# A hybrid diffusion layer: feature loads six tiles ahead, the left token block's down product in all eight banks, and weight sums formed one item early

## The chip, the cores and the metric

The kernel runs on one core of a Trainium2 chip. The metric is the device time of one execution in microseconds, the median of several runs. TensorE (PE) does the matrix products, with its weight loads shown as PEld; VectorE (DVE) and ScalarE (ACT) do the elementwise work; GpSimd (POOL) does one tiny power per row block; SyncE (SP) issues every DMA of the part spoken of here, in program order.

## The reference, cut to what matters

The layer is: a SwiGLU feed-forward block, a mixer of neighbourhood attention and a state-space scan with an output projection, and a second SwiGLU block, each followed by a residual and a layer norm. The change touches the end of the mixer (its last norm) and the whole second feed-forward block:

```python
def swiglu(h, w_up, w_down):
    a, g = jnp.split(h @ w_up, 2, axis=-1)
    return (jax.nn.silu(g) * a) @ w_down

x = post_norm(x, mod[5] * y, ln_g[layer, 1], ln_b[layer, 1])
x = post_norm(x, 0.5 * mod[8] * swiglu(modulate(x, mod[6], mod[7]), ffn2_w_up[layer], ffn2_w_down[layer]),
              ln_g[layer, 2], ln_b[layer, 2])
```

There are 1024 tokens and 1024 features in float32; the hidden width is 2816, that is 22 tiles of 128 features.

## The kernel before, in words

**Three matmuls for one.** Every float32 operand is split into a high part (ACT copies it into the matmul's format) and a low part (DVE subtracts that copy from the source; the helper `split`, L132 to L134). A product is high·high, high·low and low·high: L321 to L323 where weights are the stationary side (`mm3`), L381 to L383 where hidden features are (`token_major`).

**The weight stream.** `units` is the list of weight pieces of 128x1024 in the order of their use; `items` is the list of 128x512 operands made from them. `w_next` (L204) loads the next unit by an SP DMA into one of three `ws` buffers (some of the second block's up weights into two more, called `HX`). `w_split` (L229) makes the split of the next items, up to `ahead[0]` (usually 4) items beyond the one that PE takes now, into rings of four `wh` and four `wl` buffers; `apart` gives an item a place of its own outside the ring. `take` (L250) hands items to PE. All of this is written out in program order: an engine works through its own instructions in that order, so an instruction that waits holds up whatever stands behind it on the same engine.

**The up product of the second block.** It is computed with seven products in place of eight, over two halves of the input features, two column blocks (a and g of one hidden tile) and two token blocks of 512 (left and right). Four of a tile's seven items are plain halves of weights (1, 2, 4) or sums and differences of them: `s1` to `s4` in `seven` (L160), formed by DVE in a 128x1024 buffer `row` and then split as any other item. `ORDER` (L188) lists the (tile, item) pairs; for tiles 0 and 1 the seven are interleaved, because the right token block's sums (`RB`) are still being made then. That stretch is called the ramp here: `ramp(n)` after the n-th product runs `right1` (n = 2, 3), `right2` (n = 4, 5), `right3` (n = 6), `right4` and `right5` (n = 7). They transpose the normed right tokens on PE and form and split the block's sums on DVE and ACT. The left block's features that they need, spilled to DRAM as `xf` by `left_part`, come back by four DMAs (L1528, L1529) after the mixer's output projection. From tile 2 on, PE runs the products one after another; `gated` writes each finished hidden tile to DRAM (`hd`), high and low part, 1 MB a tile.

**The end of the mixer.** The output projection's right token block ends with `evac` (L1504): for each of four row tiles DVE multiplies by the gate (L1507), adds the residual (L1508), takes statistics (L401, L408, L410), waits for POOL's power (L411) and scales the tile (`normed`, L1494), which `turned_z` (L1544) transposes.

**The down product of the second block.** For each token block b (L1735), `token_major` runs over the two halves of the 1024 output columns, and in each over the 22 hidden tiles, with four banks (four row tiles) open at a time. All 22 hidden tiles of a block lie in SBUF (`hid_room`): `hid_load` (L1677) loads four of the left block's during the last products and the other 18 in one loop (L1700) before the first down product. After those stand the loads of the residual `z2` (L1708), two rows of norm parameters (L1711), two more (L1713). The work list `hi` has `resid2`, which DVE does in small steps when `pump` is called: z times a row (L1722), plus a row (L1724). The right block's hidden tiles replace the left's during the left block's second half (`follow`). At the end of each block every row tile's chain (L1751, L1752, statistics, POOL, L1739, L1740, store) is done at once as its banks finish (`out_now`). The weights of the down product are loaded twice, once for each token block.

```python
for j in range(4, NF):                     # L1700
    hid_load(0, j)
for t in range(4):                         # L1707
    dq.dma_start(z2[t], xh2[t])
for n, i in (("g1", 2), ("b1", 3)):
    rows[n] = rowt()
    row_load(rows[n], i)
hi += [resid2(z2[0:4]), more()]            # L1734
```

Of the kernel before, what the change touches and what calls it, by code (L numbers as in the profile page):

```python
# [48 lines left out]
def hybrid_layer(ctx: ExitStack, tc: tile.TileContext, I, out, dbg=None, stop=99):  # L49
# [110 lines left out]
    def seven(ua):  # L160
        ug = ua + 1
        h = lambda u, j: wst[u][:, j * 512:(j + 1) * 512]

        def s1():
            r = sums_of[ua] = rowt()
            V.tensor_tensor(r[:, 0:512], h(ug, 0), h(ug, 1), op=ALU.add)  # L166
            return r[:, 0:512]

        def s2():
            r = sums_of[ua][:, 0:512]  # L170
            V.tensor_tensor(r, r, h(ua, 0), op=ALU.subtract)
            return r

        def s3():
            r = sums_of[ua][:, 512:1024]
            V.tensor_tensor(r, h(ug, 0), h(ua, 0), op=ALU.subtract)
            return r

        def s4():
            r = sums_of.pop(ua)[:, 0:512]  # L180
# [14 lines left out]
    WO_END, U2 = len(items), len(units)  # L195
# [5 lines left out]
    plain(col("wd2", NF) * 2)  # L201


    def w_next(margin):  # L204
        u = pos[0]
        if u >= len(units) or (margin and u >= barred[0]):
            return False
        b = home[u][0] if u in home else turn_w[0] % NWS
        if b in owner and last_use[owner[b]] >= pos[1] - margin:
            assert margin, (u, b)  # L210
            return False
        if u in home:
# [5 lines left out]
        nc.sync.dma_start(w, units[u])  # L218
        wst[u] = w
        pos[0] += 1  # L220
        return True
# [6 lines left out]

    def w_split(n, must):  # L229
        while pos[1] < min(n, len(items)):  # L230
# [4 lines left out]
            u, f = items[i]  # L235
            if u >= barred[0] and i >= must:
                break
            w_dma(u + 1)
# [6 lines left out]
            split(wh, wl, f())  # L245
# [1237 lines left out]
    def more_units():  # L1483
# [6 lines left out]
        barred[0] = 10 ** 9  # L1490

    def normed(t, mv, rs):
        z = zz[4 + t]
        V.tensor_scalar(z, z, mv[:, 0:1], rs, op0=ALU.subtract, op1=ALU.mult)  # L1494
        dq.dma_start(xh2[4 + t], z)

    for b in range(2):
# [6 lines left out]
        def evac(hf_, t, p):  # L1504
# [3 lines left out]
            V.scalar_tensor_tensor(z, z, ALPHA, p, op0=ALU.mult, op1=ALU.add)  # L1508
            half_done(t, hf_, z)
# [16 lines left out]
    x11, x21 = pcs(ht, 0, 4), pcs(me, 0, 4)  # L1526
    for i in range(2):
        dq.dma_start(ht[:, i * 1024:(i + 1) * 1024], xf[i])  # L1528
        dq.dma_start(me[:, i * 1024:(i + 1) * 1024], xf[2 + i])  # L1529
# [8 lines left out]
          3: pair(hp[8:16]), 6: pair(hp[16:20] + ap_[0:4]), 7: pair(ap_[4:8] + spare)}  # L1538
# [28 lines left out]
    def right4(k):  # L1567
        V.tensor_tensor(x21[k], x21[k], t1f[k], op=ALU.subtract)

    def right5(k):  # L1570
        split(RB[4][0][k], RB[4][1][k], x21[k])
# [43 lines left out]
    def product(f, i):  # L1615
# [21 lines left out]
        if i == 4:  # L1637
# [9 lines left out]
    def ramp(n):  # L1647
# [6 lines left out]
        elif n == 6:  # L1654
            for k in range(4):
                right3(k)
        elif n == 7:
            for k in range(4):
                right4(k)
            hb4, a34 = slott("HB", [128, 6 * NB], F32R), slott("A3", [128, 1024], F32R)  # L1660
            RB[4] = pair(pcs(hb4, 0, 7) + pcs(a34, 0, 1))
            for k in range(4):
                right5(k)
            xe4 = slott("XE", [128, 4096])
            hring.extend([xe4[:, 0:2048], xe4[:, 2048:4096]])
# [34 lines left out]
    for j in range(4, NF):  # L1700
        hid_load(0, j)

# [3 lines left out]
    z2 = [ztile() for _ in range(4)]  # L1706
    for t in range(4):  # L1707
        dq.dma_start(z2[t], xh2[t])  # L1708
    for n, i in (("g1", 2), ("b1", 3)):
        rows[n] = rowt()  # L1710
        row_load(rows[n], i)  # L1711
    for i in range(2):
        row_load(fin[i], 4 + i)  # L1713
# [3 lines left out]
    for i in range(5):  # L1717
        apart[len(items) - 5 + i] = free[i][:, 0:512], free[i][:, 512:1024]

# [7 lines left out]
    def more():  # L1727
        for t in range(4):
            z2.append(slott(f"A{t}", [128, 1024]))
            dq.dma_start(z2[4 + t], xh2[4 + t])  # L1730
            yield None
        yield from resid2(z2[4:8])

    hi += [resid2(z2[0:4]), more()]  # L1734
    for b in range(2):  # L1735
        def out_now(t, mv, rs):
            z = z2[4 * b + t]
            for c in [slice(0, D)] if b == 0 or t < 3 else [slice(0, 512), slice(512, D)]:
                V.scalar_tensor_tensor(z[:, c], z[:, c], mv[:, 0:1], fin[0][:, c], op0=ALU.subtract, op1=ALU.mult)  # L1739
                V.scalar_tensor_tensor(z[:, c], z[:, c], rs, fin[1][:, c], op0=ALU.mult, op1=ALU.add)  # L1740
                dq.dma_start(out[4 * b + t][:, c], z[:, c])

        half_done, rest = norm(out_now)

        def src(f, t):
            return hid2[f][:, 0, t * 128:(t + 1) * 128], hid2[f][:, 1, t * 128:(t + 1) * 128]

        def evac(hf, t, p):
            c = slice(hf * 512, (hf + 1) * 512)
            z = z2[4 * b + t][:, c]  # L1750
            V.tensor_tensor(p, p, rows["g8"][:, c], op=ALU.mult)  # L1751
            V.scalar_tensor_tensor(z, z, ALPHA, p, op0=ALU.mult, op1=ALU.add)  # L1752
            half_done(t, hf, z)


        def follow():
            for _ in range(NF - 2):
                yield
            for f in range(NF):
                if f:  # L1760
                    hid_load(1, f - 1)
                yield

        fol = follow()
        token_major(NF, 4, src, evac, 2.0, (2, TAIL) if b else (2, 2), "dd", () if b else fol)
        if b == 0:
            for _ in fol:
                pass
            hid_load(1, NF - 1)
# [3 lines left out]
def layout(inp):  # L1773
# [15 lines left out]
    for i in (1, 2):  # L1789
        w = a[f"ffn{i}_w_up"][0].reshape(KD, 128, 2, NF, 128)  # L1790
        r[f"wu{i}"] = asc(w.transpose(3, 2, 1, 0, 4).reshape(2 * NF, 128, 1024))
        w = a[f"ffn{i}_w_down"][0].reshape(2, NF // 2, 128, 2, 512)
        w = w.transpose(0, 3, 1, 2, 4) if i == 1 else w.transpose(3, 0, 1, 2, 4)
        r[f"wd{i}"] = asc(w.reshape(NF, 2, 128, 512).transpose(0, 2, 1, 3).reshape(NF, 128, 1024))
    w = a["w_in"][0].reshape(KD, 128, 4, 4, 128).transpose(2, 3, 1, 0, 4).reshape(4, 4, 128, 1024)
# [48 lines left out]
```

## Time and the profile before

| | |
|---|---|
| median of 3 runs | 2274.38 us (2271.51 to 2275.09) |
| the profiled execution's own time | 2272.88 us |
| its span in the trace | 2271.0 us |
| PE busy | 2165.2 us, 95% of the span |
| DVE busy | 1595.5 us, 70% |
| ACT busy | 739.7 us, 33% |
| mean granted TensorE clock | 0.98 |

The span is the time from the first to the last instruction; the execution's own time is 1.9 us longer. PE's busy time is modelled and overlaps, so what counts below is where PE stands idle, and for what. All times of day are microseconds from the start of the span. The second feed-forward block's up product runs from about 1518 to 1970, its down product from 1970 to 2261.

### The profile page before, as it was taken

To read this page: it belongs to the slowest core of one execution; us is meant where nothing else is said; L and a number is where in the kernel's file an instruction comes from. 1 tells how busy PE (TensorE), PEld (TensorE's weight loads), DVE (VectorE), ACT (ScalarE), POOL (GpSimd) and SP (SyncE) were. 2 spreads that over 40 slices of the span, in tenths; PEclk is the share of its full clock that TensorE was granted. 3 is DMA by queue.
4 is the path that set the end of the run, shared out by engine and by line. 5 is a ranking of instruction groups with operands and counts; after the bars stand their busy time and mean duration, and the time that the engine had idled before them with its cause. 6 is when DMAs were issued, how large, how long until landed. Compare 5 with 4: busy or idle time off the path is not lost.

```text
span 2271.0 us, 32457 instructions
## 1 busy us (share of the span) xinstructions
PE 2165.2 (95%) x12272; PEld 1937.5 (85%) x12272; DVE 1595.5 (70%) x3421; ACT 739.7 (33%) x1547; POOL 24.6 (1%) x33
## 2 busy tenths in 40 slices
PE   7999999999999999999999899988999999959798
PEld 6998999889988999898999799865788888748686
DVE  7788788787888785554777467868777777543535
ACT  4322223423321333242223577234333333312121
POOL 0000000000000000000000000000000000000100
PEclk9999999999999999999999999998999999979899
DMA  9787623445444335227775871451333233485532
GB/s 344 254 295 247 253 75 117 140 168 167 124 139 131 113 125 171 93 103 240 253 250 187 202 169 37 170 208 48 130 112 112 111 112 112 160 302 190 209 102 83
DMA packets 166795, 372.30 MB, mean 164 GB/s; under 512 B 18152, under 2 KB 85736, under 8 KB 163824
## 3 DMA queue, kind: packets, MB, share of 16 engines
q1 hardware_dynamic: 166640, 370.25, 48.5%
q8 instruction: 96, 1.57, 0.3%
q14 instruction: 59, 0.48, 0.1%
HBM read 292.09 MB, written 84.06 MB: 166 GB/s over the span
## 4 chain that ended last, share of the span: by engine, by line
PE 81%; DVE 8%; DMA 5%; ACT 3%; issue 2%; SPq 1%; POOL 1%; POOLq 0%; ACTq 0%; DVEq 0%
PE pb L322 16%; PE pb L323 16%; PE pb L321 16%; PE pb L382 8%; PE pb L383 8%; PE pb L381 8%; PE pb L1337 2%; PE pb L1157 1%; DVE row L317 1%; PE pb L1312 1%; DVE wl L134 1%; ACT wh L133 1%; PE pb L1286 1%; PE pb L1287 1%; POOL rs L411 1%
## 5 line engine op out<-in xcount | busy, mean ns | idle before, releaser
L321 PE MATMUL pb<-X,wh 128*128 128x256 f32 (+2 forms) x1744 | 559.2, 321 | 1.1 <-ACT wh L133 1.1
L323 PE MATMUL pb<-X,wl 128*128 128x256 f32 (+2 forms) x1744 | 556.5, 319 | 0.0
L134 DVE TENSOR_TENSOR wl<-ws,wh 128x512 fp32r<-128x512 f32 x460 | 306.8, 688 | 267.2 <-ACT wh L133 264.8
L133 ACT ACTIVATE wh<-ws 128x512 fp32r<-128x512 f32 x460 | 281.1, 627 | 583.1 <-PE pb L383 362.0
L321 PEld LDWEIGHTS pb<-X,wh 128*128 128x128 f32 x1744 | 331.2, 190 | 10.3 <-ACT wh L133 2.0
L323 PEld LDWEIGHTS pb<-X,wl 128*128 128x128 f32 x1744 | 330.8, 190 | 9.3 <-DVE wl L134 0.9
L322 PE MATMUL pb<-X,wh 128*128 128x256 f32 (+2 forms) x946 | 307.5, 325 | 0.0
L322 PE MATMUL pb<-XT,wh 128*128 128x256 f32 (+2 forms) x886 | 284.6, 321 | 0.8 <-DVE XT L134 0.8
L381 PE MATMUL pb<-wh,HA 128*128 128x512 f32 x672 | 263.5, 392 | 2.6 <-DVE hid L350 2.1
L382 PE MATMUL pb<-wl,HA 128*128 128x512 f32 x672 | 261.5, 389 | 0.0
L322 PEld LDWEIGHTS pb<-X,wh 128*128 128x128 f32 x946 | 179.5, 190 | 7.1
L322 PEld LDWEIGHTS pb<-XT,wh 128*128 128x128 f32 x886 | 168.7, 190 | 7.4 <-DVE XT L134 2.8
L383 PE MATMUL pb<-wh,HA 128*128 128x512 f32 x416 | 162.0, 389 | 0.0
L321 PE MATMUL pb<-HA,wh 128*128 128x512 f32 (+2 forms) x424 | 154.4, 364 | 3.2 <-ACT wh L133 2.2
L323 PE MATMUL pb<-HA,wl 128*128 128x512 f32 (+2 forms) x424 | 153.3, 362 | 0.0
L381 PEld LDWEIGHTS pb<-wh,HA 128*128 128x128 f32 x672 | 126.2, 188 | 29.7 <-DVE hid L350 3.0
L382 PEld LDWEIGHTS pb<-wl,HA 128*128 128x128 f32 x672 | 126.2, 188 | 25.6
L322 PE MATMUL pb<-HA,wh 128*128 128x512 f32 (+2 forms) x336 | 118.7, 353 | 0.0
L134 DVE TENSOR_TENSOR wl<-row,wh 128x512 fp32r<-128x512 f32 x88 | 60.9, 693 | 73.3 <-ACT wh L133 73.3
L133 ACT ACTIVATE wh<-row 128x512 fp32r<-128x512 f32 x88 | 55.3, 628 | 172.1 <-DVE row L166 67.0
L383 PE MATMUL pb<-wh,HB 128*128 128x512 f32 x276 | 107.4, 389 | 0.0
L1611 DVE TENSOR_TENSOR z<-pb,z 128x512 f32<-128x512 f32 x154 | 105.7, 686 | 2.4 <-PE pb L323 0.7
(441 smaller groups left out, 3693.6 us busy)
## 6 DMA issues: line engine op xcount, KB each, us to landing
ws<-wu SPq DMA_DIRECT2D x122, 512.0 KB
ws<-wd SPq DMA_DIRECT2D x88, 512.0 KB
hd<-XE SPq DMA_DIRECT2D x22, 1024.0 KB
XE<-wada SPq DMA_DIRECT2D x36, 512.0 KB
HX<-wada SPq DMA_DIRECT2D x36, 512.0 KB
XE<-s5m SPq DMA_DIRECT2D x21, 768.0 KB
HA<-hd SPq DMA_DIRECT2D x20, 512.0 KB
HX<-wu SPq DMA_DIRECT2D x18, 512.0 KB
```

Source lines behind the costliest of these rows:

```text
L133: S.activation(h, src, AF.Copy)
L134: V.tensor_tensor(l, src, h.bitcast(F32), op=ALU.subtract)
L317: V.scalar_tensor_tensor(scr, w, 1.0, xe[:, c, :], op0=ALU.mult, op1=ALU.mult, accum_out=acc[:, m, k:k + 1])
L321: mm(p, lhsT=wh, rhs=xh, start=first, stop=False)
L322: mm(p, lhsT=wh, rhs=xl, start=False, stop=False)
L323: mm(p, lhsT=wl, rhs=xh, start=False, stop=last)
L381: mm(b[t], lhsT=h, rhs=wh, start=f + i == 0, stop=False)
L382: mm(b[t], lhsT=h, rhs=wl, start=False, stop=False)
L383: mm(b[t], lhsT=l, rhs=wh, start=False, stop=f + i == nf - 1)
L411: G.tensor_tensor(rs, rs, mhalf, op=ALU.pow)
L1337: mm(o, lhsT=p, rhs=v, start=m == 0, stop=m == len(ks) - 1)
L1611: V.tensor_tensor(o, s[i][0], x, op=ALU.add)
```

## The change

It does the following.

- **Sums early** (`source`, `w_split`). After ACT's copy of item i is issued, the next item's source is formed on DVE if its unit's load has been issued, and only then comes DVE's subtraction for item i. This holds for the second block's up items alone. `s2`, `s3` and `s4` use the halves of `row` in another order, so that a sum is not written over one that is still being read.
- **Ramp.** `ORDER` takes item 4 of tiles 0 and 1 before item 7; `right3` is now the sum for item 4 and `right4` the one for item 7, each with its four DVE operations ahead of its four splits; the banks are combined when both 4 and 7 are there. Two of the four `xf` loads are issued in `more_units`, in the middle of the output projection, into `me` (XE), and the other two after it into HB; what `right1` reads is in `me`. `normed` is put off: a row tile is scaled after the next tile's two first operations.
- **Down product.** The left block goes through the 22 hidden tiles once, both column halves of four row tiles at a time, so eight banks; the last two hidden tiles are taken row tile by row tile. Hidden loads are issued six tiles ahead in that loop, and from tile 5 on the right block's tiles five behind. The loads of `z2` and of the rows become steps of `setup2` in the work list, one each time `pump(3.5)` is called. The statistics of the left block come after the loop (`flush`), its norm and output in `rest` beside the right block's first tiles. The right block is as before, by `token_major`; its weights come as 128 x (2 x 512) pieces of two hidden tiles.

```diff
-    ORDER = [(0, 1), (0, 2), (1, 1), (1, 2), (0, 5), (1, 5), (0, 6), (1, 6), (0, 7), (1, 7), (0, 4), (0, 3), (1, 4), (1, 3)]
+    ORDER = [(0, 1), (0, 2), (1, 1), (1, 2), (0, 5), (1, 5), (0, 6), (1, 6), (0, 4), (1, 4), (0, 7), (0, 3), (1, 7), (1, 3)]
...
-    plain(col("wd2", NF) * 2)
+    DOWN = len(items)
+    plain(col("wd2", NF) + [I["wd2"][f:f + 2, :, h * 512:(h + 1) * 512].rearrange("f p c -> p f c")
+                            for h in range(2) for f in range(0, NF, 2)])
...
+    def source(i, need=True):
+        if i not in ready and i < len(items):
+            u, f = items[i]
+            if not need and (u >= pos[0] or i < U_ITEMS or i >= DOWN):
+                return
+            w_dma(u + 1)
+            ready[i] = f()
+        return ready.get(i)
...
-            split(wh, wl, f())
+            S.activation(wh, src, AF.Copy)
+            source(i + 1, False)
+            V.tensor_tensor(wl, ready.pop(i), wh.bitcast(F32), op=ALU.subtract)
...
         barred[0] = 10 ** 9
+        for i in range(2):
+            dq.dma_start(me[:, i * 1024:(i + 1) * 1024], xf[i])
...
     def normed(t, mv, rs):
-        z = zz[4 + t]
-        V.tensor_scalar(z, z, mv[:, 0:1], rs, op0=ALU.subtract, op1=ALU.mult)
-        dq.dma_start(xh2[4 + t], z)
+        def go():
+            z = zz[4 + t]
+            V.tensor_scalar(z, z, mv[:, 0:1], rs, op0=ALU.subtract, op1=ALU.mult)
+            dq.dma_start(xh2[4 + t], z)
+        scaled.append(go)
...
             V.scalar_tensor_tensor(z, z, ALPHA, p, op0=ALU.mult, op1=ALU.add)
+            while scaled:
+                scaled.pop(0)()
             half_done(t, hf_, z)
...
-    def right3(k):
-        V.scalar_tensor_tensor(x11[k], x11[k], gB[:, 1, k:k + 1], t1f[k], op0=ALU.add, op1=ALU.subtract)
-        split(RB[7][0][k], RB[7][1][k], x11[k])
...
+    def right3():
+        for k in range(4):
+            V.tensor_tensor(x21[k], x21[k], t1f[k], op=ALU.subtract)
+        for k in range(4):
+            split(RB[4][0][k], RB[4][1][k], x21[k])
+
+    def right4():
+        for k in range(4):
+            V.scalar_tensor_tensor(x11[k], x11[k], gB[:, 1, k:k + 1], t1f[k], op0=ALU.add, op1=ALU.subtract)
...
-    for j in range(4, NF):
+    for j in range(4, 6):
         hid_load(0, j)
...
+    def setup2():
+        yield None
+        for n, i in (("g1", 2), ("b1", 3)):
+            rows[n] = rowt()
+            row_load(rows[n], i)
+            yield None
+        for b in range(2):
+            for t in range(4):
+                z = ztile() if b == 0 else slott(f"A{t}", [128, 1024])
+                dq.dma_start(z, xh2[4 * b + t])
+                z2.append(z)
+                yield None
+            if b == 0:
+                for i in range(2):
+                    row_load(fin[i], 4 + i)
+                    yield None
+            yield from resid2(z2[4 * b:4 * b + 4])
...
+    acc = [[bank("d") for _ in range(2)] for _ in range(4)]
+    LAST = 2
+    for f in range(NF - LAST + 1):
+        n = 1 if f < NF - LAST else LAST
+        if f == NF - LAST - 1:
+            ahead[0] = 8
+        ws = take(2 * n)
+        for t in range(4):
+            for i in range(n):
+                h, l = hidden(f + i, t)
+                for hf in range(2):
+                    wh, wl = ws[2 * i + hf]
+                    mm(acc[t][hf], lhsT=h, rhs=wh, start=f + i == 0, stop=False)
+                    mm(acc[t][hf], lhsT=h, rhs=wl, start=False, stop=False)
+                    mm(acc[t][hf], lhsT=l, rhs=wh, start=False, stop=f + i == NF - 1)
+            if n > 1:
+                for hf in range(2):
+                    half_done(t, hf, updated(0, t, hf, acc[t][hf]))
+        if f + 6 < NF:
+            hid_load(0, f + 6)
+        if 5 <= f:
+            hid_load(1, f - 5)
+        if n == 1:
+            pump(3.5)
+    ahead[0] = 4
+    flush()
+    hi.insert(0, rest(z2[0:4], ln3_done))
...
+    token_major(NF, 4, hidden, lambda hf, t, p: half_done(t, hf, updated(1, t, hf, p)), 2.0, (2, TAIL), "dd", follow())
```

Of the functions that it calls, `ln3_done` multiplies a normed tile by one row, adds another and stores it; `updated` is the gate and the residual (the former L1751 and L1752).

## Rows read from the trace of the kernel before

**Rows 1.** The page, busy time by engine: us (share of the span) xinstructions.

```profile
PE 2165.2 (95%) x12272; PEld 1937.5 (85%) x12272; DVE 1595.5 (70%) x3421; ACT 739.7 (33%) x1547; POOL 24.6 (1%) x33
```

**Rows 2.** Timeline of PE: steady products, then first and last down matmul (start, us).

```profile
1689.81 0.39 PE L321 MATMUL pb<-HA,wh 128*128 128x512 f32 x1
...
1702.05 0.39 PE L321 MATMUL pb<-HA,wh 128*128 128x512 f32 x1
...
1970.08 0.47 PE L381 MATMUL pb<-wh,X 128*128 128x512 f32 x1
...
2261.24 0.39 PE L383 MATMUL pb<-A,XT 128*128 128x512 f32 x1
```

**Rows 3.** Table by stretch: length, busy of each engine, granted clock, DMA share, GB/s.

```profile
1900.00:1950.00 50.00, 50.00 (x222) 41.43 (x221) 37.30 (x56) 16.26 (x26) 0.00 (x0) 1.00 0.28 105
...
1984.00:2010.00 26.00, 0.00 (x0) 0.00 (x0) 0.00 (x0) 0.00 (x0) 0.00 (x0) 0.55 1.04 394
...
2014.90:2020.50 5.60, 5.59 (x13) 4.43 (x14) 5.53 (x6) 1.64 (x3) 0.00 (x0) 0.50 0.70 255
...
1559.70:1566.50 6.80, 6.60 (x13) 3.59 (x14) 5.31 (x9) 1.26 (x2) 0.00 (x0) 0.51 0.00 0
...
1526.50:1597.00 70.50, 57.33 (x213) 39.63 (x214) 53.18 (x81) 29.07 (x45) 0.00 (x0) 0.90 0.23 82
```

**Rows 4.** Whom PE waited for, 1970 to 2271: us in total, times, longest.

```profile
PE pb L382 <- DVE wl L134: 44.8, 2, 32.1
PE pb L381 <- DMA X<-hd: 1.1, 1, 1.1
```

**Rows 5.** Timeline of SP, DVE and ACT around PE's first idle stretch in the down product.

```profile
2006.55 11.66 SPq L218 DMA_DIRECT2D ws<-wd  x3
...
2011.74 1.23 DVE L1722 TENSOR_TENSOR z<-z,row 128x1024 f32<-128x1024 f32 x1 [35.63 <-DMA row<-lnr]
...
2016.88 1.15 ACT L133 ACTIVATE wh<-ws 128x512 fp32r<-128x512 f32 x2 [40.35 <-DMA ws<-wd]
```

**Rows 6.** Timeline of DVE at the end of the left token block.

```profile
2122.37 0.70 DVE L1751 TENSOR_TENSOR pb<-pb,row 128x512 f32<-128x512 f32 x1
...
2144.02 2.49 DVE L134 TENSOR_TENSOR wl<-ws,wh 128x512 fp32r<-128x512 f32 x4
```

**Rows 7.** Whom PE and DVE waited for in the ramp, 1518.3 to 1597.

```profile
PE pb L321 <- ACT wh L133: 5.0, 5, 1.7
PE pb L1544 <- DVE HB L1550: 3.5, 1, 3.5
PE pb L1544 <- DVE z L1494: 2.4, 1, 2.4
...
PE pb L322 <- DVE XT L134: 0.4, 2, 0.2
...
DVE wl L134 <- ACT wh L133: 11.1, 12, 1.6
...
DVE XT L134 <- ACT A L133: 2.8, 4, 0.7
```

**Rows 8.** Prices: timeline of ACT and DVE in the ramp, and one group by line.

```profile
1556.94 0.63 ACT L133 ACTIVATE A<-HB 128x512 fp32r<-128x512 f32 x1 [1.42 <-DVE HB L1564]
...
1525.74 0.81 DVE L1494 TENSOR_SCALAR z<-z,mv,rs 128x1024 f32<-128x1024 f32 x1 [0.73 <-POOL rs L411]
...
1502.52 1.28 DVE L404 BATCH_NORM_STATS2 st<-XE 128x6 f32<-128x512 f32 x2
...
L1722 DVE TENSOR_TENSOR z<-z,row 128x1024 f32<-128x1024 f32 x4 | 4.9, 1220 | 35.6 <-DMA row<-lnr 35.6
```

**Rows 9.** Timeline of SP, ACT and PE: the last weights of the output projection.

```profile
1501.20 0.41 SPq L218 DMA_DIRECT2D ws<-wo  x1
...
1505.19 1.15 ACT L133 ACTIVATE XT<-ws 128x512 fp32r<-128x512 f32 x2 [2.35 <-DMA ws<-wo]
...
1508.78 0.39 PE L381 MATMUL pb<-XT,HA 128*128 128x512 f32 x1
```

More of the change, by code (lines that the diff above doesn't have):

```diff
@@ L194, in hybrid_layer @@
     plain(col("wg", 2) + col("wo", 8) * 2)
-    WO_END, U2 = len(items), len(units)
+    U_ITEMS = WO_END = len(items)
+    U2 = len(units)
     for f in range(NF):
@@ L217, in w_next @@
         owner[b] = u
-        nc.sync.dma_start(w, units[u])
+        nc.sync.dma_start(w if len(units[u].shape) == 2 else w.rearrange("p (f c) -> p f c", f=2), units[u])
         wst[u] = w
@@ L234, in w_split @@
                 break
-            u, f = items[i]
-            if u >= barred[0] and i >= must:
+            if items[i][0] >= barred[0] and i >= must:
                 break
-            w_dma(u + 1)
+            src = source(i)
             if i in apart:
@@ L1525, in hybrid_layer @@
     ht = slott("HB", [128, 6 * NB])
-    x11, x21 = pcs(ht, 0, 4), pcs(me, 0, 4)
+    x11, x21 = pcs(me, 0, 4), pcs(ht, 0, 4)
     for i in range(2):
-        dq.dma_start(ht[:, i * 1024:(i + 1) * 1024], xf[i])
-        dq.dma_start(me[:, i * 1024:(i + 1) * 1024], xf[2 + i])
+        dq.dma_start(ht[:, i * 1024:(i + 1) * 1024], xf[2 + i])
+    scaled.pop(0)()
     ta = slott("A3", [128, 1024])
@@ L1561, in right2 @@
             split(RB[3][0][k], RB[3][1][k], x)
-    def right3(k):
-        V.scalar_tensor_tensor(x11[k], x11[k], gB[:, 1, k:k + 1], t1f[k], op0=ALU.add, op1=ALU.subtract)
-        split(RB[7][0][k], RB[7][1][k], x11[k])
[L1567 to L1571, printed above, removed]
+    def right3():
[6 more added lines that the diff above has]
+            V.scalar_tensor_tensor(x11[k], x11[k], gB[:, 1, k:k + 1], t1f[k], op0=ALU.add, op1=ALU.subtract)
+        hb4, a34 = slott("HB", [128, 6 * NB], F32R), slott("A3", [128, 1024], F32R)
+        RB[7] = pair(pcs(hb4, 0, 7) + pcs(a34, 0, 1))
+        for k in range(4):
+            split(RB[7][0][k], RB[7][1][k], x11[k])
+        xe4 = slott("XE", [128, 4096])
+        hring.extend([xe4[:, 0:2048], xe4[:, 2048:4096]])
     st2 = {}
@@ L1636, in product @@
             add(A[:, hi_], s, 5, A[:, hi_], False)
-        if i == 4:
+            s["u3"] = True
+        if i in (4, 7) and 4 in s and "u3" in s:
             add(B[:, lo], s, 4, B[:, hi_])
@@ L1654, in ramp @@
         elif n == 6:
[L1655 to L1665, printed above, removed]
+            right3()
+        elif n == 8:
+            right4()
     hid_room = []
@@ L1705, in hybrid_layer @@
     fin = [hx[:, 0:1024], hx[:, 1024:2048]]
[L1706 to L1713, printed above, removed]
+    z2 = []
     xe = slott("XE", [128, 4096], F32R)
@@ L1718, in hybrid_layer @@
         apart[len(items) - 5 + i] = free[i][:, 0:512], free[i][:, 512:1024]
+        if i < 4:
+            apart[DOWN + 2 * NF - 4 + i] = apart[len(items) - 5 + i]
     def resid2(zs):
@@ L1725, in resid2 @@
             yield 1.2
-    def more():
-        for t in range(4):
[L1729 to L1769, printed above, removed]
@@ new lines, in hybrid_layer, with updated, ln3_done @@
+    hi.append(setup2())
+    hidden = lambda f, t: [hid2[f][:, i, t * 128:(t + 1) * 128] for i in range(2)]
+    def updated(b, t, hf, p):
+        c = slice(hf * 512, (hf + 1) * 512)
+        z = z2[4 * b + t][:, c]
+        V.tensor_tensor(p, p, rows["g8"][:, c], op=ALU.mult)
+        V.scalar_tensor_tensor(z, z, ALPHA, p, op0=ALU.mult, op1=ALU.add)
+        return z
+    def ln3_done(t, z):
+        V.tensor_tensor(z, z, fin[0], op=ALU.mult)
+        V.tensor_tensor(z, z, fin[1], op=ALU.add)
+        dq.dma_start(out[t], z)
@@ new lines, in hybrid_layer @@
+    half_done, rest = norm()
+    acc = [[bank("d") for _ in range(2)] for _ in range(4)]
[5 more added lines that the diff above has]
+        ws = take(2 * n)
+        for t in range(4):
+            for i in range(n):
[14 more added lines that the diff above has]
+            pump(3.5)
@@ new lines, in hybrid_layer, with out_now @@
+    ahead[0] = 4
+    flush()
+    hi.insert(0, rest(z2[0:4], ln3_done))
+    def out_now(t, mv, rs):
+        z = z2[4 + t]
+        for c in [slice(0, D)] if t < 3 else [slice(0, 512), slice(512, D)]:
+            V.scalar_tensor_tensor(z[:, c], z[:, c], mv[:, 0:1], fin[0][:, c], op0=ALU.subtract, op1=ALU.mult)
+            V.scalar_tensor_tensor(z[:, c], z[:, c], rs, fin[1][:, c], op0=ALU.mult, op1=ALU.add)
+            dq.dma_start(out[4 + t][:, c], z[:, c])
+    half_done, rest = norm(out_now)
@@ L1770, in hybrid_layer, with follow @@
+    def follow():
+        for f in range(NF - LAST - 4, NF):
+            hid_load(1, f)
+            yield
+    token_major(NF, 4, hidden, lambda hf, t, p: half_done(t, hf, updated(1, t, hf, p)), 2.0, (2, TAIL), "dd", follow())
     drain()
```

16 lines of the change are left out of this document (9 added, 7 removed).

## The prediction

> **What bounds the kernel now.** I read the page's busy shares first. PE has 95% of the span [rows 1], so a gain can only come from PE's idle time and from its slow time. I then went through PE's waits and the table by stretch, only where the change works: the ramp (1518 to 1597), the steady products (to 1970), the down product (to 2261).
>
> *Steady products.* Between the first two matmuls shown there are 54 starts in 12.24 us, 0.2267 us each [rows 2]. PE is busy all of a 50 us stretch at the full clock while DVE has 37.3 us [rows 3]. PE bounds it; nothing on DVE can gain here.
>
> *Down product.* It has 22 tiles x 8 row tiles x 2 halves x 3 = 1056 matmuls; 1055 starts at 0.2267 us are 239.2 us. From the first start to the last there pass 291.2 us [rows 2]. So 52 us are lost: 45.9 us waiting, nearly all in two waits for a low part `wl` [rows 4], the rest at half clock behind these. Behind the first wait the granted clock is 0.50 for 5.6 us, 13 matmuls [rows 3]; behind the second it is so for 5.4 us. Half of 11.0 us is 5.5 us lost, and 45.9 + 5.5 = 51.4.
>
> The first wait (32.1 us): DVE stood in L1722 for a row of norm parameters until 2011.7, and the `wl` that PE wanted stands behind it; ACT stood until 2016.9 for weights that SP could issue only at 2006.55 [rows 5]. SP had first issued 18 hidden tiles, four residual tiles and four rows. From 1984 to 2010 the DMA engines were full, at 394 GB/s, with no engine computing [rows 3]. So this is a queue order, not a lack of weights. The second wait (12.7 us): DVE ran four row tiles' chains from 2122.4 to 2144.0, and `wl` stood behind them [rows 6].
>
> *Ramp.* PE waits eight kinds of things between 5.0 and 0.4 us [rows 7]; they add to 15.1 us. Twice the clock is at half, for 5.6 us (1533.6 to 1539.2) and 6.8 us [rows 3], which loses 6.2 us more. DVE is the engine behind most of it: busy 53.2 of 70.5 us [rows 3], idle mainly for ACT's copies, 11.1 and 2.8 us [rows 7].
>
> **The down product after the change.** *Left block.* A tile now has 4 x 2 x 3 = 24 matmuls, 5.44 us. The 32.1 and 1.1 us go if everything arrives in time. What was issued ahead of the weights is now spread out: one weight unit a tile, one hidden tile six ahead, from tile 5 one of the right block, and one residual tile or row at a `pump`. Counting the `pump` steps: rows g1 and b1 at tiles 1 and 2, z0 to z3 at 3 to 6, the other two rows at 7 and 8, `resid2` at 9 to 11, z4 to z7 at 11 to 14, `resid2` at 15 to 17. DVE's L1722 thus comes at least three tiles, 16 us, behind the load it reads; had that cover gone, it would block `wl` as before. DVE's load is two `wl` (1.4 us) and three steps of 1.22 us [rows 8], 5.1 of 5.44 us in the worst tile: it fits.
>
> The traffic: 23 weight units, 32 hidden tiles, eight residual tiles and four rows, 67 x 0.524 MB = 35.1 MB in 119.7 us, 293 GB/s. Tiles 5 to 15 are tightest: 33 + 8 = 41 loads, 21.5 MB in 59.8 us, 359 GB/s, against the 394 GB/s that the full queue moved [rows 3]. At that rate they need 54.6 us. A weight unit is issued some two tiles before its split. I cost the traffic at nothing.
>
> On this the Trainium skill speaks against the change: Perfetto Trace Analysis, section Roofline, gives a core 358 GB/s of HBM, though a single active core may pull more. By 358 GB/s tiles 5 to 15 would need 60.0 us, 0.2 us over their matmuls, and the margin would be gone. The measured 394 GB/s decides here.
>
> *Its end.* This is where I expect the next stall. PE takes the last two tiles row tile by row tile, 12 matmuls, 2.72 us each; DVE needs four operations of 0.70 to 0.73 us for each, 2.9 us, and so ends some 3.4 us behind PE. `flush` adds eight statistics at 0.64 us (half of 1.28) [rows 8], 5.1 us. Four items (two hidden tiles' worth of ring) were split ahead, so the right block's first four tiles, 10.9 us, go through. The fifth `wl` stands in DVE's order behind the statistics, four small chains (about 1.6 us), POOL's first power and the first tile's scaling: 0.81 [rows 8] + 2 x 1.22 = 3.3 us. That is 3.4 + 5.1 + 1.6 + 0.5 + 3.3 + 0.7 = 14.6 us against the 11.1 us at which PE wants it: 3.5 us. For the next three tiles DVE has 3.3 + 0.6 = 3.9 us and PE 2.72: 1.2 us each. In all 7.1 us. Nothing else is late there: the first banks of the right block were emptied during the tail. For the clock I take the same loss as behind the earlier waits, 2.8 us. Bounds: nothing, and the 12.7 + 2.7 us of the second wait now.
>
> Down product: 52.0 - 7.1 - 2.8 = **42 us gained**. The end of the kernel (the right block's last chains) is the same.
>
> **The ramp after the change.** *`xf` early.* `right1` no longer waits for the DMA that holds PE 3.5 us [rows 7]. The price: two loads of 512 KB now stand in SP's queue ahead of the projection's last weights, and the second must wait for the spill that SP issued just before, at 1500.2. I shift the weights by 2.5 us: issue 1501.20, ACT 1505.19, so 1507.7; the low parts some 1.2 us later at most touch PE's first use at 1508.78 [rows 9]. Between 0 and 3 us, I take 1, because the DVE chains of the four row tiles start from there.
>
> *`normed` put off.* POOL's power holds DVE 0.73 us a row tile [rows 8]; two operations of 0.7 us now lie over it for three of four tiles. PE's wait of 2.4 us [rows 7] shrinks by some 1 to 2 us.
>
> *Batches and early sums.* In the old `right3` each piece went DVE, ACT, DVE in turn; the 1.42 us of ACT's idle time [rows 8] and 0.7 us of DVE's, four times, go. Twelve waits of DVE for ACT's copy, 11.1 us [rows 7], are partly filled with the next sum: the sums are 10 of these items, at 0.7 us each. No operation is added. If DVE's idle time falls from 17.3 to about 5 us, its 53.2 us end 12 us earlier; PE itself needs some 53 us for the same, so DVE and PE then end about together, with some small waits and perhaps one stretch at half clock left. Of 15.1 + 6.2 = 21.3 us I let 10 stay. With the 1 us of the weights that is 11.3 - 1 = **10 to 11 us gained**; bounds 4 (only the DMA's wait goes) and 17.
>
> In the steady products a sum one item earlier could only hurt if its unit had not landed; neither DVE nor ACT waits for a weight there, so nothing.
>
> **The sum.** 42 + 11 = 53 us. The profiled execution took 2272.9 us, its span 2271.0, so 2219.9; the median of the runs is 1.5 us above the profiled one: **2221 us**.
>
> **The rivals.**
> *The left block is held by its loads* (a weight unit or a residual tile comes late, and DVE blocks `wl` again). For it: 359 GB/s wanted is 91% of the best seen, in one queue and in order. Against it: leads of two to six tiles. If tiles 5 to 15 got three quarters of the best rate, 296 GB/s, 21.5 MB would take 72.6 us, 13 more than PE; some 8 us of lead cover part of it, and two stretches at half clock add 5.6: about 10 us lost, **2231 us**. Chance 0.12.
> *The ramp gains nothing*, since DVE is its bound and only changes what it waits for: 42 us alone, **2232 us**. Chance 0.13.
> *The end of the left block costs nothing and the ramp goes well*: 52 + 15 us, **2207 us**. Chance 0.07.
> *Slower than before*: SP's order chains the loads, every hidden tile waiting behind a store or a weight buffer that waits for DVE, so that the whole left block runs at the queue's pace. It turns slower when 35.1 MB take more than 119.7 + 53 us, below 203 GB/s. At half of the full queue's rate, 197 GB/s, the block takes 178 us: 58 us lost, **2279 us**. The stretch in which the queue was full shows twice that rate [rows 3]. Chance 0.03.
> *The change only moves the waits*: DVE's residual steps stay ahead of `wl` and cost the same 45 us, leaving a weak ramp's gain of 4: **2270 us**. Chance 0.02.
>
> **The numbers.** The forecast has 0.63. The range from 2208 to 2236 takes in the boundary's bounds (-10, +5) and the ramp's (-6, +7), the first two rivals with some of their spread, and leaves out the extremes. A measurement of this kernel can tell about 0.2%, 4.5 us, from no change. The last rival lies within that, the one before it beyond it on the other side, all other cases are gains: faster 0.95, same 0.02, slower 0.03.
>
> **What would show it.** PE's wait of 32 us for `wl` gone, no wait of DVE for the rows, ACT not waiting for `ws<-wd`; the DMA rate spread at 290 to 390 GB/s over 1960 to 2080; one group of waits for `wl` of 1 to 4 us behind the left block, behind L404 and `rest`; no wait for HB<-xf in the ramp and DVE's idle time there cut. The forecast is wrong if PE waits in the middle of the left block, if the ramp still has over 15 us of waits and slow clock, or if the steady products show any wait.

## The result, and the profile after

| | before | after |
|---|---|---|
| median of 4 runs, same chip | 2272.95 us (2271.46 to 2275.09) | 2211.59 us (2209.75 to 2213.49) |
| ratio, 95% interval | | **0.9729** [0.9713, 0.9746] |
| the profiled execution's own time, and span | 2272.88, 2271.0 us | 2211.69, 2209.6 us |

The change takes 61.4 us away; 53 had been forecast. The time is inside the range, 9 us under the point. One execution of `flood`, a kernel below, took 2405.84 us at a granted clock of 0.85; it is left out of that kernel's median, and since it was the profiled one, no line of its trace is used.

Where did the gain come from? Four marks cut the span, all read from PE's timeline: the projection's first and last matmul, and the first and last matmul of the down product. The same cuts are made in every kernel below. "Ramp" here is the stretch from the last projection matmul to the first down matmul; it holds the ramp and the steady products, which are the same matmuls in all kernels.

| us | projection | ramp + products | down | after it | span |
|---|---|---|---|---|---|
| before | 102.9 | 452.0 | 291.2 | 9.8 | 2271.0 |
| after | 104.7 | 435.5 | 243.8 | 9.8 | 2209.6 |
| gain | -1.8 | 16.6 | 47.4 | 0.0 | 61.4 |

The rest (-0.6) lies ahead of the projection, where the code is the same and the start of the projection scatters by some us between executions. So small steps are read from these stretches, not from spans. Each stretch is read from one execution; between kernels whose code is the same there, the ramp + products agree within 0.5 us and the down product within 0.1 us.

PE's share and the down product's two ends, from the page and PE's timeline of the kernel after:

```profile
PE 2154.9 (98%) x12272; PEld 1933.3 (87%) x12272; DVE 1597.0 (72%) x3425; ACT 739.1 (33%) x1547; POOL 22.0 (1%) x33
...
1955.97 0.47 PE L1793 MATMUL pb<-wh,X 128*128 128x512 f32 x1
...
2199.76 0.39 PE L399 MATMUL pb<-A,XT 128*128 128x512 f32 x1
```

Against [rows 1], the busy times of PE, DVE and ACT have changed by half a per cent or less: what went is PE's idle and slow time. 243.8 us are 4.6 over the 239.2 that 1055 starts at 0.2267 us need.

The waits of PE in the kernel after; first 1970 to 2210 (all that it has there), then the ramp, 1515 to 1600 (total us, times, longest):

```profile
PE pb L398 <- DVE wl L261: 3.4, 4, 0.9
...
PE pb L337 <- ACT HB L133: 3.3, 1, 3.3
PE pb L337 <- ACT wh L259: 1.5, 2, 0.9
PE pb L338 <- DVE HB L134: 0.7, 1, 0.7
PE pb L338 <- DVE XT L134: 0.5, 1, 0.5
PE pb L338 <- DVE A L134: 0.5, 2, 0.2
PE pb L1569 <- DVE HB L1575: 0.2, 1, 0.2
```

The first line answers to [rows 4]: 45.9 us in three waits became 3.4 in four. The others answer to [rows 7]: 15.1 us became 6.7.

The windows of the kernel after (length, busy of PE, PEld, DVE, ACT, POOL, granted clock, DMA share, GB/s): the left block's tightest 60 us, the boundary behind it, the only slow clock left in the ramp, and the ramp's middle:

```profile
1980.00:2000.00 20.00, 20.00 (x90) 16.57 (x89) 4.33 (x7) 4.63 (x8) 0.00 (x0) 1.00 1.04 398
2000.00:2020.00 20.00, 20.00 (x89) 16.54 (x89) 14.63 (x16) 4.23 (x7) 0.00 (x0) 1.00 1.04 397
2020.00:2040.00 20.00, 20.00 (x90) 16.56 (x89) 6.25 (x9) 5.06 (x8) 0.00 (x0) 1.00 1.03 395
...
2085.00:2100.00 15.00, 11.65 (x47) 8.35 (x47) 14.76 (x17) 1.78 (x3) 1.39 (x2) 1.00 0.71 248
...
1559.30:1562.80 3.50, 3.46 (x8) 2.75 (x9) 3.50 (x6) 1.48 (x3) 0.00 (x0) 0.52 0.04 9
...
1540.00:1560.00 20.00, 14.98 (x60) 10.62 (x59) 19.83 (x33) 10.91 (x20) 0.00 (x0) 0.98 0.15 53
```

In [rows 3] the queue moved 394 GB/s while no engine computed; now it moves 395 to 398 GB/s for 60 us with PE 100% busy at the full clock. That is the picture of a gain from order alone.

### The profile page after: what moved, and what is told of

Same layout as the page of the kernel before. It is cut to its first block, busy times and chain, and to the rows that moved or that the text cites. A ratio compares the mean times of both kernels' runs of the same rounds, so it can differ in the third digit from the quotient of the medians.

```text
span 2209.6 us, 32479 instructions
## 1 busy us (share of the span) xinstructions
PE 2154.9 (98%) x12272; PEld 1933.3 (87%) x12272; DVE 1597.0 (72%) x3425; ACT 739.1 (33%) x1547; POOL 22.0 (1%) x33
## 5 line engine op out<-in xcount | busy, mean ns | idle before, releaser
L397 PE MATMUL pb<-wh,HA 128*128 128x512 f32 x592 | 232.4, 393 | 2.0 <-DVE hid L366 1.4
L398 PE MATMUL pb<-wl,HA 128*128 128x512 f32 x592 | 230.5, 389 | 0.8 <-DVE wl L261 0.8
L397 PEld LDWEIGHTS pb<-wh,HA 128*128 128x128 f32 x592 | 111.2, 188 | 26.0 <-DVE hid L366 2.3
L398 PEld LDWEIGHTS pb<-wl,HA 128*128 128x128 f32 x592 | 111.2, 188 | 23.5 <-DVE wl L261 1.2
L399 PE MATMUL pb<-wh,HA 128*128 128x512 f32 x336 | 130.9, 389 | 0.0
L399 PE MATMUL pb<-wh,HB 128*128 128x512 f32 x252 | 98.1, 389 | 0.0
L337 PEld LDWEIGHTS pb<-HA,wh 128*128 128x128 f32 x424 | 79.8, 188 | 11.5 <-ACT wh L259 1.1
L339 PEld LDWEIGHTS pb<-HA,wl 128*128 128x128 f32 x424 | 79.8, 188 | 10.6 <-DVE wl L261 0.4
```

The costliest lines, as they stand in the source:

```text
L337: mm(p, lhsT=wh, rhs=xh, start=first, stop=False)
L339: mm(p, lhsT=wl, rhs=xh, start=False, stop=last)
L397: mm(b[t], lhsT=h, rhs=wh, start=f + i == 0, stop=False)
L398: mm(b[t], lhsT=h, rhs=wl, start=False, stop=False)
L399: mm(b[t], lhsT=l, rhs=wh, start=False, stop=f + i == nf - 1)
```

## The experiments

All times are medians; ratios are to the kernel before on the same chip. Five of the intervals (`ten_ahead`, `left_at_once`, `pieces`, `norm_at_once`, `xf_late`) overlap with that of the kernel after, 0.9713 to 0.9746; for these the stretches are the evidence, not the whole times.

| run | us | ratio [95%] | ramp + products | down |
|---|---|---|---|---|
| down_only | 2224.23 | 0.9797 [0.9782, 0.9812] | 451.9 | 243.8 |
| spread_only | 2242.61 | 0.9876 [0.9862, 0.9891] | 451.9 | 263.4 |
| flood | 2234.07 | 0.984 [0.982, 0.986] | | |
| ten_ahead | 2215.81 | 0.9759 [0.9745, 0.9772] | 435.9 | 250.3 |
| left_at_once | 2216.58 | 0.9759 [0.9743, 0.9775] | 435.4 | 252.8 |
| sums_late | 2218.62 | 0.9768 [0.9750, 0.9786] | 443.4 | 243.8 |
| pieces | 2213.75 | 0.9746 [0.9730, 0.9763] | 438.6 | 243.8 |
| norm_at_once | 2214.52 | 0.9748 [0.9732, 0.9764] | 438.5 | 243.8 |
| xf_late | 2207.46 | 0.9716 [0.9702, 0.9731] | 435.5 | 243.8 |
| paced_late | 2202.36 | 0.9699 [0.9685, 0.9712] | 435.9 | 239.2 |
| paced_late_r7 | 2202.57 | 0.9697 [0.9684, 0.9711] | 435.5 | 239.2 |

**The down product alone: do the two parts add up?** The kernel before, with the new down product and nothing else (its `ORDER`, ramp and sums as before).

> The kernel before with the down product's part of the change alone. If the two parts are independent, this keeps the 47.4 us that lie between the first and the last down matmul of the two traces (291.2 against 243.8 us) and loses all of the ramp's gain: about 2226 us. The rival: part of the down product's gain hangs on the early sums, because DVE is freer at the seam; then 2230 us or more.

Measured: ramp + products 451.9 us, as before (452.0), and down 243.8 us, as after (243.8). The parts are independent and add.

**The spread alone.** The kernel before, its two passes of four banks kept, with the hidden loads and the residual's loads spread as in the change:

```diff
-    for j in range(4, NF):
+    for j in range(4, 6):
         hid_load(0, j)
...
+        if f + 6 < NF:
+            hid_load(0, f + 6)
...
-    hi += [resid2(z2[0:4]), more()]
+    hi.append(setup2())
```

> The kernel before with only its loads spread: hidden tiles six ahead, residual tiles and rows by the pump; two passes of four banks and the chains at the end of the left block stay. Theory (the order in the queue made the first wait): the 32.1 us wait and 1.1 us go, with 2.8 us at half clock, the second wait of 12.7 us stays: 2237 us. Rival (the pass over both halves is needed, since a tile of 2.72 us with a hidden tile, half a weight unit and a residual tile asks 482 GB/s, over the 394 seen): PE waits 5 to 15 us in the first pass, 2242 to 2255 us.

Measured: 2242.61 us, on the border between the two. PE's waits of this kernel in the down product, ACT's there, and the window in which its loads were densest:

```profile
PE pb L382 <- DVE wl L134: 14.6, 2, 12.7
PE pb L381 <- DMA HA<-hd: 2.3, 3, 0.8
PE pb L381 <- DMA X<-hd: 0.8, 1, 0.8
...
ACT wh L133 <- DMA ws<-wd: 63.9, 10, 22.4
...
1985.00:2005.00 20.00, 18.43 (x80) 14.67 (x79) 3.99 (x7) 3.46 (x6) 0.00 (x0) 1.00 1.03 399
```

The 32.1 us of [rows 4] are gone by the order of issue alone, worth 27.8 us of the stretch (291.2 to 263.4). What is left is the second wait, 12.7 us, which this kernel was meant to keep, and five small ones, 5.1 us: a half pass is 2.72 us a tile and draws the left block's hidden tiles in half the time, so the queue is full at 399 GB/s and still slightly late: ACT waits ten times for weights. The other 19.6 us (263.4 to 243.8) come from the single pass with eight banks and the norm put off, which no run here takes apart fully; `left_at_once`, below, prices the norm alone at 9.0 within the single pass. Neither account was right alone: the spread removes the stall, the single pass gives it the time to be spread over.

**The flood put back.** The new down product, with all left hidden loads issued ahead of it as before:

```diff
-    for j in range(4, 6):
+    for j in range(4, NF):
         hid_load(0, j)
...
-        if f + 6 < NF:
-            hid_load(0, f + 6)
```

> The changed kernel with all 18 hidden loads of the left block ahead of its first down tile. Theory (queue order): the fourth weight unit stands behind some 24 us of loads and lands near 1988, while PE wants it near 1972: PE waits about 15 us once, and half clock adds 2.8 us: 2230 us. Rival (the one pass with eight banks is what pays, its tiles of 5.44 us cover the queue): 2212 us, no wait over 2 us in the left block.

Measured: 22.5 us over the kernel after (three runs, 2230.95 to 2237.98), where 18 were forecast and the rival had none. The one-pass loop alone does not give the gain; the order in the queue does. Where PE waited in these three runs is not shown.

**Ten ahead in place of six.** How near is six to a limit? `range(4, 6)` became `range(4, 10)` and `f + 6` became `f + 10`.

> The changed kernel with hidden loads ten tiles ahead in place of six, so four more loads of 1.3 us before the loop. Theory (the queue's order sets the fourth weight unit's landing, which in the changed kernel is about 1 us before PE wants it): one wait of about 4 us at the fourth tile, some half clock: 2216 us. Rival (there is slack enough in the queue): 2212 us.

Measured: 4.2 us slower; the down product takes 6.5 us more. PE's only new wait in this kernel, and ACT's copy behind it in ACT's timeline (in brackets: idle before, and who ended it):

```profile
PE pb L1793 <- ACT wh L259: 4.6, 1, 4.6
...
1971.62 1.15 ACT L259 ACTIVATE wh<-ws 128x512 fp32r<-128x512 f32 x2 [14.04 <-DMA ws<-wd]
```

Most of the rest of the 6.5 us is the slow clock behind that wait (a window, columns as above):

```profile
1972.00:1975.50 3.50, 3.20 (x7) 2.28 (x8) 1.88 (x3) 1.92 (x4) 0.00 (x0) 0.51 1.04 402
```

The same copies in ACT's timeline of the kernel after:

```profile
1970.06 1.16 ACT L259 ACTIVATE wh<-ws 128x512 fp32r<-128x512 f32 x2 [7.65 <-DMA ws<-wd]
1973.74 1.15 ACT L259 ACTIVATE wh<-ws 128x512 fp32r<-128x512 f32 x2 [2.52 <-DMA ws<-wd]
1977.59 1.16 ACT L259 ACTIVATE wh<-ws 128x512 fp32r<-128x512 f32 x2 [2.70 <-DMA ws<-wd]
1982.80 1.31 ACT L259 ACTIVATE wh<-ws 128x512 fp32r<-128x512 f32 x2 [4.06 <-PE pb L1795]
```

After the change ACT, too, waits three times for the weights, 12.9 us in all. From the first down matmul at 1955.97, three tiles of 5.44 us end at 1972.3: the copy for the fourth ends at 1971.2. So six ahead has about 1 us to spare at that tile. For the next two the same sum gives 2.8 and 4.4 us, and at 1982.80 the releaser is PE again: the lead is regained. Four more loads ahead of that weight, 2 MB or 5.3 us at 395 GB/s, use it up.

**The left block's norm done at once.** What is `flush` and `rest` worth? Each row tile's chain again directly behind its banks, with the two fused operations that the kernel before used:

```diff
-    half_done, rest = norm()
+    half_done, rest = norm(out_left)
...
                     half_done(t, hf, updated(0, t, hf, acc[t][hf]))
+                    flush()
...
-    hi.insert(0, rest(z2[0:4], ln3_done))
```

> The changed kernel with the left block's norm done row tile by row tile as its banks finish, as before. Theory (the low part waits behind whatever DVE has in front of it): some 7.6 us of DVE a row tile against 2.72 us of PE, DVE 22 us behind when PE ends the block, four items split ahead cover 11 us: one wait of about 11 us for wl, and half clock of 2.7 us behind it, in place of 3.4 us: 2222 us. Rival (PE's wait there comes from the banks, not from DVE's order): 2212 us.

Measured: 5.0 us slower, the down product 9.0 us longer. Windows of this kernel, PE's one wait and what follows it, and DVE's timeline at its end:

```profile
2085.90:2096.10 10.20, 0.00 (x0) 0.00 (x0) 9.11 (x14) 0.42 (x1) 2.25 (x2) 0.60 0.13 51
2096.20:2101.60 5.40, 5.40 (x13) 4.24 (x14) 1.67 (x3) 0.00 (x0) 0.00 (x0) 0.50 0.92 302
...
2095.38 2.49 DVE L261 TENSOR_TENSOR wl<-ws,wh 128x512 fp32r<-128x512 f32 x4
```

It is the second wait of [rows 4] again, a little shorter, with the 5.4 us at half clock behind it: 10.2 + 2.7 - 3.4 = 9.5, of which 9.0 appear. The four `wl` stand behind all of the block's chains, as in [rows 6].

**The sums at their old place.** Only the line that forms the next source early is taken out:

```diff
             S.activation(wh, src, AF.Copy)
-            source(i + 1, False)
             V.tensor_tensor(wl, ready.pop(i), wh.bitcast(F32), op=ALU.subtract)
```

> The changed kernel without the early sums: each sum is formed when its own item is split, as before. Theory (in the ramp DVE is the bound and idles for ACT's copies, 11.1 us before): DVE's idle time grows by 4 to 7 us there and PE's waits with it, nothing changes in the steady products: 2216 to 2219 us. Rival (PE's waits in the ramp come from the block's sums alone): 2212 us.

Measured: 7.0 us slower, ramp + products 8.0 us longer. DVE's waits in the ramp, first of this kernel (1528.9 to 1600), then of the kernel after (1528.9 to 1583):

```profile
DVE wl L260 <- ACT wh L259: 12.7, 14, 1.6
```

```profile
DVE wl L261 <- ACT wh L259: 3.9, 5, 1.1
```

The wait of [rows 7], 11.1 us, is back in full. On PE it arrives more as slow clock than as waits: its waits in the ramp grow only from 6.7 to 9.7 us, but three stretches of this kernel, 13.6 us in all against 3.5 us in the kernel after, ran at half clock, which is some 5 us of the 8:

```profile
1547.80:1551.20 3.40, 3.40 (x9) 2.29 (x8) 3.40 (x7) 1.71 (x4) 0.00 (x0) 0.50 0.01 2
1561.50:1568.30 6.80, 5.92 (x13) 4.35 (x14) 5.32 (x9) 3.22 (x6) 0.00 (x0) 0.50 0.25 78
1585.40:1588.80 3.40, 3.29 (x8) 2.57 (x9) 2.52 (x3) 0.78 (x2) 0.00 (x0) 0.50 0.59 243
```

The early sums are the ramp's largest single part.

**`right3` piece by piece.** The second loop over `k` is taken out, so that subtraction and split alternate:

```diff
         for k in range(4):
             V.tensor_tensor(x21[k], x21[k], t1f[k], op=ALU.subtract)
-        for k in range(4):
             split(RB[4][0][k], RB[4][1][k], x21[k])
```

> The changed kernel with right3 done piece by piece, each piece's subtraction, copy and low part in turn. Theory: DVE waits some 0.7 us for ACT's copy in each of four pieces, 2.8 us, which pass to PE since DVE is busy all through the stretch: 2214 to 2215 us. Rival (two products of 5.4 us lie between right3 and the product that reads it, and hide it): 2212 us.

Measured: ramp + products 3.1 us longer. Its time is 2.2 us over the kernel after, less than the runs can tell apart, so the stretch decides. The size is as forecast, the way is not. DVE's four waits are there, 2.8 us, but they do not pass to PE as waits: PE waits 5.7 us in this ramp and 6.7 in that of the kernel after. What grew is the time at half clock, from 3.5 to 10.2 us in two stretches, worth 3.4 us. DVE's waits, then windows of this kernel: a stretch in which PE had four waits of 0.22 to 0.53 us, and right behind it the longer of the two at half clock:

```profile
DVE XT L134 <- ACT A L133: 2.8, 4, 0.7
...
1551.70:1555.50 3.80, 2.49 (x8) 0.97 (x6) 2.42 (x4) 1.26 (x2) 0.00 (x0) 0.99 0.00 0
1555.50:1562.30 6.80, 6.49 (x15) 4.43 (x14) 6.03 (x11) 1.78 (x3) 0.00 (x0) 0.50 0.16 45
```

**`normed` at once.** `scaled.append(go)` became `go()`, and the last `scaled.pop(0)()` fell away.

> The changed kernel with each right row tile scaled at once, DVE waiting for POOL's power. Theory: 0.73 us of DVE waiting in three row tiles, 2.2 us, of which PE sees what its first transposes wait for: 2213 to 2214 us. Rival (hidden behind the two products that PE does before the transposes): 2212 us.

Measured: 2.9 us slower, ramp + products 3.0 us longer. PE's wait for the normed tile in this kernel, 1510 to 1600:

```profile
PE pb L1568 <- DVE z L1516: 2.7, 1, 2.7
```

The 2.4 us of [rows 7] are back.

**The early `xf` loads put back behind the projection.** The two loads into `me` are issued next to those into `ht`, as before:

```diff
         barred[0] = 10 ** 9
-        for i in range(2):
-            dq.dma_start(me[:, i * 1024:(i + 1) * 1024], xf[i])
...
     for i in range(2):
+        dq.dma_start(me[:, i * 1024:(i + 1) * 1024], xf[i])
         dq.dma_start(ht[:, i * 1024:(i + 1) * 1024], xf[2 + i])
```

> The changed kernel with all four spilled feature loads after the output projection. Theory: PE's wait of 3.4 us for them comes back with 2.8 us at half clock, the 1.1 us wait for the projection's last weights goes; in all 3 to 5 us slower: 2215 to 2217 us. Rival (the loads in the queue ahead of the weights cost as much as they save): 2212 us.

Measured: 2207.46 us, not slower, as the forecast had it, but 4.1 us below the kernel after. The ratios' intervals overlap, so the whole times do not settle the difference; the stretches do. Ramp + products are the same (435.5), so the early issue brings nothing; and the projection takes 102.9 us where it took 104.7. Over all kernels the split is clean: 102.8 to 103.0 us in the six with the loads behind the projection, 103.6 to 105.0 in the six with them in it, 1.2 us more on average. What else there is in the 4.1 us lies outside these stretches, in scatter.

Why is the 3.5 us wait of [rows 7] gone without them? SP's queue, first in the kernel before, then in `xf_late`:

```profile
1522.55 4.35 SPq L1495 DMA_DIRECT2D xh<-z  x2
1526.99 0.38 SPq L1528 DMA_DIRECT2D HB<-xf  x1
```

```profile
1521.23 0.32 SPq L1515 DMA_DIRECT2D xh<-z  x1
1521.60 0.42 SPq L1551 DMA_DIRECT2D XE<-xf  x1
...
1523.96 0.42 SPq L1515 DMA_DIRECT2D xh<-z  x1
```

Before, the load stood behind the last two stores of normed tiles, which wait for DVE: 4.35 us for the pair. With the last tile's scaling written behind the loads, its store (1523.96) stands behind them too, and they go some 5 us sooner. By this order in the queue the deferred `normed` was the cure; no run puts both back.

The price that the early loads take is in the timelines of SP, ACT and PE of the kernel after:

```profile
1501.99 2.09 SPq L1508 DMA_DIRECT2D XE<-xf  x2
1504.17 0.38 SPq L221 DMA_DIRECT2D ws<-wo  x1
...
1509.89 1.15 ACT L259 ACTIVATE XT<-ws 128x512 fp32r<-128x512 f32 x2 [6.34 <-DMA ws<-wo]
...
1510.58 0.50 PE L397 MATMUL pb<-XT,HA 128*128 128x512 f32 x1 [0.93 <-ACT XT L259]
```

The last weights are copied at 1509.89 in place of 1505.19 [rows 9], and PE waits 0.93 us for them.

**Both leftovers removed.** `xf_late`, and the steps of `rest` behind the left block set further apart, so that each weight split comes between two of them:

```diff
-        def rest(zs, done):
+        def rest(zs, done, us=(0.3, 1.6)):
...
-                yield 0.3
+                yield us[0]
...
-                yield 1.6
+                yield us[1]
...
-    hi.insert(0, rest(z2[0:4], ln3_done))
+    hi.insert(0, rest(z2[0:4], ln3_done, (0.5, 4.0)))
```

> The changed kernel with all four spilled loads after the output projection (as in xf_late) and the left block's norm paced at what it costs: one row tile in every second tile of the right block. Theory (the four waits of 0.83 to 0.87 us behind the left block are DVE's norm steps standing ahead of wl): all four go, 3.4 us below xf_late: 2204 us. Rival (they are the eight statistics' doing): one wait of 1 to 3 us stays, 2206 us.

Measured: 2202.36 us, the fastest with the next one, 9.2 us under the kernel after. PE has no wait for `wl` left in the down product; its first and last matmul:

```profile
1951.60 0.47 PE L1792 MATMUL pb<-wh,X 128*128 128x512 f32 x1
...
2190.84 0.39 PE L399 MATMUL pb<-A,XT 128*128 128x512 f32 x1
```

They lie 239.24 us apart, which is 1055 x 0.2267: at that pace, the steady products' own, this stage has nothing more to give without fewer matmuls. Of the 9.0 us between the two spans, 4.6 come from here and 1.8 from the projection, 0.4 are lost in the ramp; the other 3.0 lie ahead of the projection and are scatter.

**And `right4` one product sooner.** On top of `paced_late`, `elif n == 8:` became `elif n == 7:`, against the last 3.3 us of the ramp.

> The same with right4 one product earlier. Theory (PE's 3.3 us wait in the ramp is right4 standing behind two additions, a sum and a split in DVE's order): that wait falls to about 1 us and the half clock behind it goes: 2201 us. Rival (DVE is full there, and what is put first only makes another item late): 2204 us, with new waits for wh in the ramp.

Measured: 2202.57 us, the same. PE's waits of this kernel in the ramp:

```profile
PE pb L337 <- ACT wh L259: 3.8, 2, 2.9
PE pb L339 <- DVE wl L261: 1.4, 1, 1.4
```

In place of one wait for `HB` come waits for `wh` and `wl`. In the kernel after DVE is busy 19.83 of 20 us there (1540 to 1560, above), so an earlier piece only makes another late.

## Why the prediction was right

- **The left block's waits** (forecast: 32.1 + 1.1 us and the half clock behind go). They went; no wait of PE stands inside the block. "A queue order, not a lack of weights" is shown by `flood` and by `spread_only`. Two of the signs named did not come: ACT did wait for `ws<-wd`, and the queue ran at 395 to 398 GB/s for 60 us where 290 to 390 had been named. Both belong to the next point.
- **"I cost the traffic at nothing."** Right in the sum, since PE lost nothing in it, but "a weight unit is issued some two tiles before its split" hid how little was left: about 1 us at the fourth tile. The first loads, not tiles 5 to 15, were the tight place, and `ten_ahead` falls over there. On the rate, the queue held these 395 to 398 GB/s. The trace agrees here with the Trainium skill (Perfetto Trace Analysis, Roofline), by which 358 GB/s is a core's share while both cores of a pair are active, and a core that is active alone can pull more. So that page did not speak against the change, as the prediction has it.
- **The boundary** (7.1 us and 2.8 us of slow clock forecast; 3.4 us of waits and no slow clock measured): the mechanism was right, with waits of 0.82 to 0.87 us for `wl` at the four places named. DVE's last statistics and the `wl` for the fifth tile, and the first two waits:

```profile
2077.95 4.84 DVE L420 BATCH_NORM_STATS2 st<-z 128x6 f32<-128x512 f32 x8
...
2087.16 0.68 DVE L261 TENSOR_TENSOR wl<-ws,wh 128x512 fp32r<-128x512 f32 x1
...
2087.90 0.50 PE L398 MATMUL pb<-wl,X 128*128 128x512 f32 x1 [0.87 <-DVE wl L261]
...
2091.74 0.50 PE L398 MATMUL pb<-wl,X 128*128 128x512 f32 x1 [0.83 <-DVE wl L261]
```

  From one such start to the next there pass 3.84 us where a tile needs 2.72: each wait costs 1.1 us, more than the idle time shown, and the four make up nearly all of the 4.6 us by which the stretch misses 239.2. So the three later waits (1.2 each forecast) were sized right, and the first term was mis-sized: 3.5 us forecast, 1.1 measured. DVE ended 2.0 us behind PE rather than 3.4; the statistics took 4.8 us (forecast 5.1), the chains 1.2 (1.6), and POOL's power held nobody (0.5). That makes 11.9 in place of 14.6 us against the 11.1 that PE allowed. The clock's loss was taken from waits of 12.7 us and more; behind these it stayed at 1.00. Together 5.3 us too much was charged, as the stretch shows (47.4 against 42). The rival that put this end at nothing was nearer than the forecast, by little.
- **The ramp** (10 to 11 us; 16.6 - 1.8 = 14.8 measured). The step that failed is "of 15.1 + 6.2 = 21.3 us I let 10 stay", and both numbers in it. One and the same matmul of the steady products, 336.48 us ahead of the first down matmul in both kernels and the 400th behind the projection's last, before and after:

```profile
1633.60 0.39 PE L322 MATMUL pb<-A,wh 128*128 128x512 f32 x1
```

```profile
1619.49 0.39 PE L338 MATMUL pb<-A,wh 128*128 128x512 f32 x1
```

  From the projection's last matmul that is 115.5 us before and 99.0 after; 400 starts at 0.2267 us are 90.7. So 24.8 us were lost there before, not 21.3, and 8.3 stay, not 10 (both are lower bounds, since the short transposes among the 400 need less). At least a part of what the 21.3 lacked is that, as at the boundary, a wait costs more than the idle time that the trace gives for it. What stays is 6.7 us of waits and, at 0.52 for 3.5 us, 1.7 of clock. The early sums alone gave 8.0 us, batching 3.1 and the deferred norm 3.0. These are measured by undoing one at a time, so they need not add up to the whole; 2.4 of the 16.6 us were assigned to none of them. The new `ORDER` and the batch in `right4` were not undone by any run.
- **"`right1` no longer waits for the DMA"** came true for a reason other than the one named: the last store's place in SP's queue, not the early loads. The price named was the right kind. The last weights came 4.7 us later, where 2.5 was the estimate, and the projection lost 1.8 us, 1.2 on the average of six kernels (1 taken, 0 to 3 given).
- **The steady products** showed no wait, as said, and took the same time in both kernels.

So the sum came out 8 us short by two terms that were mis-sized to the same side: the boundary by 5.4, the ramp by some 4 (0.6 went the other way ahead of the projection). A further 1 us lies in the start: the forecast began at a median of three runs, 2274.4, where four gave 2273.0. The time lies between the forecast and the rival at 2207 us, in which both terms go well, and it is nearer to that rival, which had been given a chance of 0.07. The mechanisms named were the ones at work, but for the early `xf` loads; their sizes were not, and it is the range that holds the measured time, not the point.

## What to carry to other kernels

Before calling a transfer late, see what stands ahead of it in its queue and what its consumer's engine does first: here 47 us were won from the same bytes, matmuls and DVE work. Put the load that is wanted first ahead of a store that waits for an engine, and spread bulk loads to the pace of their consumption, but measure how much lead they leave the weights: six tiles ahead held by about 1 us and ten did not. Undo each part of a change by itself, since one of them (the early `xf` loads) cost the projection 1.2 us and won nothing, while the others won.

## What the runs showed of the hardware that was not expected

The core's DMA queue moved 395 to 398 GB/s in three 20 us windows on end with PE 100% busy beside it, against 394 with no engine computing, so the matmuls cost it nothing.

In these runs the granted clock did not go by the length of the single wait. Four waits of 0.82 to 0.87 us, some 3.9 us apart, left it at 1.00; in `pieces` four waits of 0.22 to 0.53 us within 3.8 us, with PE busy for 2.49 us of these, were followed by 6.8 us at 0.50, the lower of its two levels. The wait of 3.3 us in the ramp was followed by 3.5 us at 0.52, and one of 10.2 us by 5.4 us at 0.50. The price in clock is therefore not to be scaled from one wait to another: it has to be read from the granted clock, also where the table of waits shows no growth.
